# A two-layer fp32 encoder trunk on one core: other routes for weight parts, rotations and sums around TensorE

## The chip, the cores and the metric

The kernel runs on one core of a Trainium2 chip. The core has five engines that each work through a queue of instructions in order: PE (matmul, with its weight loads PEld), DVE (VectorE), ACT (ScalarE), POOL (GpSimd) and SP, which here only issues loads and stores. DMAs are issued from SP's queue (plain loads) or from POOL's (those that add to what lies at the destination). The metric is the time of one execution in microseconds on the device, the median of several runs.

## The reference, cut to what matters

Two layers on x of 512 tokens by 1024, with a memory of 256 tokens, all in fp32. Layer 0 has two token mixers side by side, layer 1 two others (latent attention C, neighbourhood attention D); each layer goes on with cross attention into the memory and a SwiGLU network of width 2816.

```python
def mixer_ab(h, w_in, g_qa, g_ka, sink, w_out, ang_1d, ang_2d):
    qa, ka, va, qb, kb, vb = _split(h @ w_in, AB_SIZES)          # 512,128,128,512,128,128
    qa = apply_rope(rms_norm(qa.reshape(B, S, 8, 64), g_qa), ang_2d)
    ka = apply_rope(rms_norm(ka.reshape(B, S, 2, 64), g_ka), ang_2d)
    oa = blocked_dense_attention(qa, ka, va, HEAD_DIM ** -0.5)   # A: dense
    qb, kb = apply_rope(qb, ang_1d), apply_rope(kb, ang_1d)      # B: no norm
    ob = window_attention_with_sink(qb, kb, vb, sink, HEAD_DIM ** -0.5)
    return jnp.concatenate([oa, ob], axis=-1) @ w_out

for i in range(DEPTH):                                           # 2
    x = x + mixer(rms_norm(x, g_mix[i]))                         # ab, then cd
    x = x + memory_cross_attention(rms_norm(x, g_xq[i]), rms_norm(mem, g_mem[i]), ...)
    g, u = jnp.split(rms_norm(x, g_ffn[i]) @ w_gate_up, 2, axis=-1)
    x = x + (jax.nn.silu(g) * u) @ w_down
return rms_norm(x, g_final)
```

A rotation multiplies a head of 64 by cosines and adds the swapped halves of 32 multiplied by sines. The norm of a head is one factor per token and head, so it may be applied before or after the rotation.

## The kernel before

Every fp32 product is made of three matmuls on a high and a low part of each operand (`mm3`, lines 140 to 142). The high part is the value cast to a shorter format, the low part the rest. So each weight that is loaded (`raw`, by SP) is turned into `wh` and `wl`. `split` (line 117 ACT cast, line 123 subtraction on DVE or, in four pieces, on POOL) does it on the engines. `split_by_dma` (lines 132 to 134) casts the high part, writes the negated value into `wl` with its rounding, and lets a DMA of POOL's queue add the weight from memory to it, which spares the subtraction.

A tile framework orders the instructions of each engine ahead of time by its own simulated schedule; on the chip each engine follows that order and waits on semaphores. PSUM has banks named `mm`, `s`, `t` (two buffers each), `x` and `o` (one each).

Layer 0's mixer (`mixer_ab`): A's keys and values are projected at the start, A's queries and all of B's by `natural`, which fills two `mm` banks for each weight load with 48 matmuls of 256 columns each. `rotate` copies a bank to SBUF (ACT, line 433), squares and sums it for A (POOL line 422, DVE lines 424 and 427), multiplies with cosine on POOL (line 382) and sine on DVE (lines 383 and 384), adds (line 385). The result is cut into high and low (lines 489 and 490), transposed on PE into the one `X` bank (line 447) and copied to a stack by ACT (line 449). Attention runs in units of one head and half of the rows, in three steps (scores, maxima, exponentials; transposes `T` of the weights with ACT line 293 and DVE line 294; products `O`), as a software pipeline (`pipeline`). B's projections are work without waits that the schedule lays between A's attention steps. Then follow two output projections (`out_proj`) and the keys and values of the memory.

The SwiGLU network takes 18 of its 22 column tiles with seven products in place of eight (`left_factors` makes seven left factors from four quarters of a loaded weight, `winograd` multiplies, `pc` and `u` are its partial sums in SBUF, lines 1150 to 1157). Quarters A11, A12 and A22 are themselves left factors (`loaded`, lines 1109 to 1111: two ACT operations and a DMA of 256 KB that adds), four others are sums (`parts`: ACT cast line 1102, DVE subtraction line 1103). Down projections come in three groups (tiles 0 to 7, 8 to 15, 16 to 21). In layer 0 `by_columns` also reorders the tokens of the eight x tiles (ACT line 1172, DVE line 1173). `last_step` makes the final norm in two halves of 256 tokens; the sum of squares is gathered in SBUF and summed over partitions by four small matmuls (line 163).

Of the kernel before, what the change touches and what calls it, by code (L numbers as in the profile page):

```python
# [17 lines left out]
P = 128  # L18
# [13 lines left out]
def trunk_kernel(  # L32
# [30 lines left out]
    def x_bank():  # L63
        return bank_of("X", 1)
# [192 lines left out]
    def softmax_rows(tiles, reduce_max, neg, extra=None):  # L257
# [11 lines left out]
        nc.vector.reciprocal(ri, ssum)  # L269
# [107 lines left out]
    def rope_mul(ph, dst, src, cv, sv, nh):  # L377

        t1 = dst
        t2 = src[1]  # L380
        s = src[0]
        nc.gpsimd.tensor_mul(t1, s, cv)
        nc.vector.tensor_mul(t2[:, :, 0:32], s[:, :, 32:64], sv[:, :, 0:32])
        nc.vector.tensor_mul(t2[:, :, 32:64], s[:, :, 0:32], sv[:, :, 32:64])
        alternate("rot").tensor_add(t1, t1, t2)

    def mixer_ab(after):
# [6 lines left out]
        with tc.tile_pool(name="ab", bufs=2) as ph:  # L394
# [34 lines left out]
            def rotate(src3, scale, cs, tt, nh, norm):  # L429
# [994 lines left out]
```

## Time and profile before

| | us |
|---|---|
| median of 3 runs | 1384.22 (1384.17 to 1385.93) |
| the profiled execution | 1384.54 |
| its span, first to last instruction | 1382.7 |
| PE busy | 1346.1 |
| DVE busy | 981.9 |
| ACT busy | 794.0 |
| POOL busy | 427.9 |

Around the span lie 1.8 us. The mean granted clock of TensorE over the span is 0.993 of full speed. Busy time is the time in which an engine works on some instruction; a busy PE may still work at a lower clock.

### The profile page before, as it was taken

The numbers are of one execution on the slowest core, as the hardware profiler recorded it, in microseconds if no ns is written. First come the engines' busy times: TensorE is split into PE (matmuls) and PEld (weight loads), VectorE is DVE, ScalarE is ACT, GpSimd is POOL, SyncE is SP. The second block draws the span as 40 slices with busy tenths as digits, with TensorE's granted clock in tenths as the row PEclk, the third lists the DMA queues.
The fourth block names the chain that finished last, engine by engine and source line by source line (L and its number), as shares of the span: only waits on it lengthen the run. The fifth ranks groups of instructions, "written<-read, shape, count | busy, mean of one in ns | idle before, by whom it ended". The sixth has DMA issues, their size and how long they took to land.

```text
span 1382.7 us, 24067 instructions
## 1 busy us (share of the span) xinstructions
PE 1346.1 (97%) x9131; PEld 1231.4 (89%) x9131; DVE 981.9 (71%) x1909; ACT 794.0 (57%) x1584; POOL 427.9 (31%) x536
## 2 busy tenths in 40 slices
PE   8998999999999999999999999999999999999997
PEld 8887889998998998898988887798989989998997
DVE  6998886769766785685569656547698766856765
ACT  5467775657643673473468557456567526743543
POOL 4855445212212221210213446642122122212111
PEclk9999999999999999999999999999999999999998
DMA  7110023311862874552222336145207636744721
GB/s 239 62 62 32 1 92 122 123 62 24 198 160 77 199 175 129 133 142 82 79 66 63 73 86 159 38 132 164 72 9 171 173 107 159 179 136 117 181 69 62
DMA packets 98317, 152.45 MB, mean 110 GB/s; under 512 B 7631, under 2 KB 71066, under 8 KB 92570
## 3 DMA queue, kind: packets, MB, share of 16 engines
q1 hardware_dynamic: 77418, 118.93, 26.7%
q0 software_dynamic: 20784, 31.99, 14.2%
q8 instruction: 72, 1.18, 0.3%
q14 instruction: 43, 0.35, 0.1%
HBM read 148.80 MB, written 2.10 MB: 109 GB/s over the span
## 4 chain that ended last, share of the span: by engine, by line
PE 77%; DVE 8%; DMA 6%; ACT 4%; issue 3%; SPq 1%; POOL 1%; POOLq 0%; ACTq 0%; DVEq 0%
PE mm L140 12%; PE mm L141 12%; PE mm L142 12%; PE S L1141 8%; PE mm L1141 5%; PE T L1141 5%; PE O L568 2%; DMA raw<-in_w_gate_up_dram 2%; PE S L140 2%; DMA wl<-in_w_gate_up_dram 2%; PE S L141 2%; PE T L290 2%; PE S L142 2%; PE T L141 1%; PE T L140 1%
## 5 line engine op out<-in xcount | busy, mean ns | idle before, releaser
L117 ACT CAST wh<-raw 128x1024 fp32r<-128x1024 f32 (+3 forms) x125 | 123.0, 987 | 137.2 <-PE mm L141 46.3
L123 DVE TENSOR_TENSOR wl<-raw,wh 128x1024 fp32r<-128x1024 f32 (+3 forms) x115 | 139.8, 1217 | 23.3 <-ACT wh L117 21.6
L271 POOL TENSOR_SCALAR P<-P,sm 128x512 f32<-128x512 f32 (+2 forms) x128 | 82.1, 661 | 79.7 <-DVE sm L269 55.9
L141 PE MATMUL mm<-act,wh 128*128 128x512 f32 (+1 forms) x264 | 98.9, 375 | 0.0
L142 PE MATMUL mm<-act,wl 128*128 128x512 f32 (+1 forms) x264 | 98.7, 375 | 0.0
L1111 POOL DMA_DIRECT2D wh<-in_w_gate_up_dram x54 | 46.9, 868 | 167.1 <-ACT wh L1110 106.1
L140 PE MATMUL mm<-act,wh 128*128 128x512 f32 (+1 forms) x264 | 98.3, 376 | 0.0
L1141 PE MATMUL S<-bf,wl 128*128 128x256 f32 x648 | 87.7, 284 | 1.7 <-DVE pc L1157 1.7
L1141 PE MATMUL S<-bf,wh 128*128 128x256 f32 x648 | 86.2, 283 | 0.0
L1141 PEld LDWEIGHTS S<-bf,wl 128*128 128x128 f32 x648 | 82.0, 192 | 2.4 <-DVE pc L1157 2.1
L1141 PEld LDWEIGHTS S<-bf,wh 128*128 128x128 f32 x648 | 81.9, 192 | 0.5
L1111 POOL DMA_DIRECT2D wl<-in_w_gate_up_dram x54 | 47.2, 873 | 112.8 <-ACT wl L1110 44.1
L1117 DVE TENSOR_TENSOR ws<-raw 128x512 f32<-128x512 f32 x72 | 49.5, 688 | 43.3 <-DMA raw<-in_w_gate_up_dram 43.2
L140 PE MATMUL mm<-wh,xgh 128*128 128x256 f32 (+1 forms) x256 | 74.1, 290 | 3.0 <-ACT rt L433 2.3
L156 POOL TENSOR_TENSOR P<-P 128x512 f32<-128x512 f32 (+1 forms) x21 | 26.3, 1253 | 154.8 <-ACT P L152 154.8
L1102 ACT CAST wh<-ws 128x512 fp32r<-128x512 f32 x72 | 44.6, 619 | 50.2 <-PE mm L141 17.7
L141 PE MATMUL mm<-wl,xgh 128*128 128x256 f32 (+1 forms) x256 | 73.1, 286 | 0.0
L142 PE MATMUL mm<-wh,xgl 128*128 128x256 f32 (+1 forms) x256 | 73.0, 286 | 0.0
L1274 POOL TENSOR_TENSOR x<-x,P 128x512 f32<-128x512 f32 x16 | 24.9, 1559 | 154.8 <-DVE P L1273 154.8
L294 DVE TENSOR_TENSOR ptl<-T,pth 128x512 fp32r<-128x512 f32 (+2 forms) x96 | 58.1, 616 | 14.4 <-ACT pth L293 14.2
L1109 ACT CAST wh<-raw 128x512 fp32r<-128x512 f32 x54 | 33.6, 622 | 53.2 <-PE mm L141 23.6
L293 ACT CAST pth<-T 128x512 fp32r<-128x512 f32 (+2 forms) x96 | 49.5, 536 | 24.8 <-PE T L290 24.4
(424 smaller groups left out, 4754.1 us busy)
## 6 DMA issues: line engine op xcount, KB each, us to landing
raw<-in_w_gate_up_dram SPq DMA_DIRECT2D x44, 1024.0 KB, 5.5
raw<-in_w_down_dram SPq DMA_DIRECT2D x16, 1024.0 KB, 5.6
wl<-in_w_gate_up_dram POOLq DMA_DIRECT2D x54, 256.0 KB, 5.7
wh<-in_w_gate_up_dram POOLq DMA_DIRECT2D x54, 256.0 KB, 5.7
raw<-in_w_xkv_dram SPq DMA_DIRECT2D x8, 1024.0 KB, 5.2
raw<-in_w_down_dram SPq DMA_DIRECT2D x8, 768.0 KB, 5.0
raw<-in_w_in_ab_dram SPq DMA_DIRECT2D x5, 1024.0 KB, 6.5
raw<-in_w_out_ab_dram SPq DMA_DIRECT2D x4, 1024.0 KB, 5.1
```

The source lines that it names most:

```text
L117: nc.scalar.copy(hv, v)
L123: low.tensor_sub(lv[:, q], v[:, q], hv[:, q].bitcast(F32))
L140: nc.tensor.matmul(o, lh, rh, start=start, stop=False)
L141: nc.tensor.matmul(o, lh, rl, start=False, stop=False)
L142: nc.tensor.matmul(o, ll, rh, start=False, stop=stop)
L271: nc.gpsimd.tensor_scalar(p, p, ri[:, j:j + 1], 1.0, op0=ALU.mult, op1=ALU.mult)
L293: nc.scalar.copy(hv, tv)
L294: nc.vector.tensor_sub(ptl[:, k0:k1, j * P:(j + 1) * P], tv, hv.bitcast(F32))
L1102: nc.scalar.copy(hl[:, 0], x)
L1111: nc.gpsimd.dma_start(hl[:, 1], src[:, i], accum_op=ALU.add)
L1117: nc.vector.tensor_tensor(t, x, y, op=op)
L1141: nc.tensor.matmul(bank, x, y, start=start and k == 0 and i == 0, stop=k == n - 1 and i == 2, skip_group_check=True)
```

## The change

Seven edits, in the order of the program. In the rows below a number behind a name tells buffers apart, a row's waits stand in brackets, and line numbers behind the changed helper functions differ by a few between the two kernels.

1. `rotate` takes the sine products directly from the PSUM bank (`scalar_tensor_tensor`, with the token's factor in it), its squares for A by ACT from the bank, and applies the norm after the rotation; POOL's squares go.
2. B's three `natural_weights` take `split_by_dma`: six ACT operations and six DMAs of 512 KB in place of six DVE subtractions. The first of them, for B's keys and values, is issued behind A's last `pow` and last stack copy.
3. `out_proj` in layer 0 splits its even halves on DVE alone and its odd halves by DMA; before, DVE and POOL alternated.
4. `memory_normed` of layer 0 has its squares and their sum behind the exponentials and sums of B's unit 5.
5. A22 is made by `parts` in place of `loaded`.
6. `by_columns` is spread over tiles 16 to 19, two x tiles each.
7. In `last_step` the last two tiles' squares go to the small matmuls without the sum in SBUF before.

```diff
+    def natural_weights(w, c0, eng=None, n=256, by_dma=False):
...
+        return [split_by_dma(v[:, k], 4, n, src[:, k]) if by_dma else split(v[:, k], 4, n, eng) for k in ks]
...
-    def out_proj(os_, w, r0, after=None, by_dma=False):
+    def out_proj(os_, w, r0, after=None):
...
-                if by_dma and mq:
-                    wh, wl = split_by_dma(v[:, :, cq], nk, 256, src[:, :, cq])
-                else:
-                    wh, wl = split(v[:, :, cq], nk, 256, None, nc.vector if by_dma else alternate("op"))
+                wh, wl = split_by_dma(v[:, :, cq], nk, 256, src[:, :, cq]) if mq else split(v[:, :, cq], nk, 256)
...
-            def headnorm(qn, scratch, nh):
-                nc.gpsimd.tensor_mul(scratch, qn, qn)
-                ss = small(nh)
-                nc.vector.tensor_reduce(ss, scratch, axis=AX, op=ALU.add)
-                ri = small(nh)
-                rsqrt_mean(ri, ss, 64, nh)
-                nc.vector.tensor_mul(qn, qn, ri.unsqueeze(2).broadcast_to([P, nh, 64]))
...
+                nc.scalar.activation(v, src, AF.Copy, scale=scale)
+                if norm:
+                    sq = tmp()[:, :nh * 64].rearrange("p (h d) -> p h d", h=nh)
+                    nc.scalar.activation(sq, src, AF.Square, scale=scale)
+                nc.gpsimd.tensor_mul(t1, v, cv)
+                for a, b in ((slice(0, 32), slice(32, 64)), (slice(32, 64), slice(0, 32))):
+                    nc.vector.scalar_tensor_tensor(t2[:, :, a], src[:, :, b], scale, sv[:, :, a],
+                                                   op0=ALU.mult, op1=ALU.mult)
...
-                    natural(xh, xl, w_in, c0, evac)
+                    with tc.issue_after(dense["pow"]), tc.issue_after(dense["stack"]):
+                        parts = natural_weights(w_in, c0, by_dma=True)
+                    natural(xh, xl, w_in, c0, evac, parts)
...
-                natural(xh, xl, w_in, c0, evac, natural_weights(w_in, c0, nc.gpsimd) if isA and c0 == 0 else None)
+                natural(xh, xl, w_in, c0, evac,
+                        natural_weights(w_in, c0, nc.gpsimd if isA and c0 == 0 else None, by_dma=not isA))
...
+        with queued("exp"):
+            for i in range(4):
...
-        r["A22"] = loaded(3)
+        r["A22"] = parts(a22)
...
-                if layer == 0 and j == NF - 2:
-                    by_columns(ph)
+                if layer == 0 and 16 <= j < 20:
+                    by_columns(ph, (2 * j - 32, 2 * j - 31))
...
+        if m < KF - 2:
+            sum_sq(st["acc"], xm, m)
+        else:
+            sq = tmp()[:, :256]
+            nc.scalar.activation(sq, xm, AF.Square)
...
+            for a in (st["acc"], sq) if m == KF - 2 else (sq,):
+                for t in range(2):
+                    nc.tensor.matmul(st["sums"][t], a[:, t * P:(t + 1) * P], ones[:, 0:1],
+                                     start=a is st["acc"], stop=m == KF - 1)
```

How the order moves, first on PE in layer 0's mixer. `mm_759` (before) and `mm_769` (after) are the last bank of A's query projection, `X` the transposes for the stacks, `mm_1516` and `mm_1530` the first bank of B's keys and values. Before:

```order
L141 MATMUL mm_759<-wl_662,xgh_210 128x256
L142 MATMUL mm_759<-wh_661,xgl_211 128x256
L447 MATMUL X_547<-identr_84,nst_514 128x128 [waits DVE_49,Activation_49]
L140 MATMUL mm_1516<-wh_1508,xgh_132 128x256 [waits Activation_49]
L141 MATMUL mm_1516<-wl_1509,xgh_132 128x256
L142 MATMUL mm_1516<-wh_1508,xgl_133 128x256
L140 MATMUL mm_1516<-wh_1508,xgh_142 128x256
```

After, the end of the same projection and what follows:

```order
L141 MATMUL mm_769<-wl_670,xgh_210 128x256
L142 MATMUL mm_769<-wh_669,xgl_211 128x256
L439 MATMUL X_559<-identr_84,nst_518 128x128 [waits Activation_49]
L439 MATMUL X_559<-identr_84,nst_518 128x128 x3
L505 MATMUL S_865<-K_353,Q_457 128x512
L506 MATMUL S_865<-K_353,Q_457 128x512
L505 MATMUL S_869<-K_353,Q_457 128x512
L506 MATMUL S_869<-K_353,Q_457 128x512
```

After, 41 rows further on (five more such pairs of scores are among the rows between), where B's projection begins:

```order
L567 MATMUL O_969<-ptl_920,vst_352 128x256
L140 MATMUL mm_1530<-wh_1520,xgh_132 128x256 [waits Activation_49]
L140 MATMUL mm_1612<-wh_1520,xgh_132 128x256
L141 MATMUL mm_1530<-wl_1521,xgh_132 128x256 [waits DMASW0_49]
L142 MATMUL mm_1530<-wh_1520,xgl_133 128x256
L140 MATMUL mm_1530<-wh_1520,xgh_142 128x256
L141 MATMUL mm_1530<-wl_1521,xgh_142 128x256
```

Before, one stack's transpose stands between A's last projection and B's first, and A's scores come later. After, all of A's stacks, seven pairs of scores (`S`), four groups of transposes (`T`) and a group of products (`O`) stand there, and the second matmul of `mm_1530` waits for a DMA.

On ACT after, where B's first two weight loads (`raw_1518`, `raw_1696`) are turned into parts; `Q_662<-X_859` is A's last stack, `P` are exponentials:

```order
L262 ACTIVATE P_904,sm_910<-S_901,sm_909 128x512 [waits DVE_49,Activation_49]
L441 CAST Q_662<-X_859 128x2x256 [waits PE_49]
L132 CAST wh_1520<-raw_1518 128x1024 [waits DMAHW6_49]
L133 ACTIVATE wl_1521<-raw_1518 128x1024
L132 CAST wh_1525<-raw_1518 128x1024
L133 ACTIVATE wl_1526<-raw_1518 128x1024
L132 CAST wh_1698<-raw_1696 128x1024 [waits DMAHW3_49]
L133 ACTIVATE wl_1699<-raw_1696 128x1024
L132 CAST wh_1703<-raw_1696 128x1024
L292 CAST pth_953<-T_955 128x4x128 [waits PE_49]
L133 ACTIVATE wl_1704<-raw_1696 128x1024
L262 ACTIVATE P_908,sm_910<-S_905,sm_909 128x512 [waits DVE_49,Activation_49]
```

And on POOL after, the DMAs that add to those parts:

```order
L270 TENSOR_SCALAR P_890<-P_890,sm_893 128x512 [waits DMAHW2_49,Activation_49]
L134 DMA wl_1521<-in_w_in_ab_dram 128x4x256 [waits Activation_49]
L134 DMA wl_1526<-in_w_in_ab_dram 128x4x256 [waits Activation_49]
L134 DMA wl_1699<-in_w_in_ab_dram 128x4x256 [waits Activation_49]
L134 DMA wl_1704<-in_w_in_ab_dram 128x4x256 [waits Activation_49]
L270 TENSOR_SCALAR P_904<-P_904,sm_911 128x512 [waits DMAHW1_49,DVE_49]
L270 TENSOR_SCALAR P_908<-P_908,sm_911 128x512 [waits DMAHW3_49,Activation_49]
```

All eight weight operations, with one cast of `pth` among them, stand between A's last stack and the third unit's second exponential; the four DMAs stand ahead of that unit's scaling on POOL. Before, each of these weight pieces has one operation on ACT, one subtraction on DVE and no such DMA.

On DVE around the reordering of tokens, before, where all eight stand among the seven-product tiles (six more are in the 15 rows behind):

```order
L1117 TENSOR_TENSOR ws_7344<-raw_7319,ws_7327 128x512
L1157 TENSOR_TENSOR pc_7080<-pc_7080,S_7078 128x256
L1173 COPY x0_90<-perm_7457 128x512
L1103 TENSOR_TENSOR wh_7208<-ws_7206,wh_7208 128x512
L1223 TENSOR_TENSOR g_7169<-pc_7080,T_7079 128x256
L1173 COPY x1_91<-perm_7460 128x512
L1226 TENSOR_TENSOR g_7169<-pc_7080 128x256
```

And after, where six of them stand among the down projection of the group before (lines 1277 and 1278), and the last two 20 rows further on:

```order
L1278 TENSOR_TENSOR x5_95<-x5_95,P_6832 128x512
L1107 TENSOR_TENSOR wl_6920<-ws_6909,wl_6920 128x512
L1177 COPY x4_94<-perm_7187 128x512
L1177 COPY x5_95<-perm_7190 128x512
L1277 TENSOR_TENSOR P_6866<-mm_6837,bc_4337 128x512
L1107 TENSOR_TENSOR wh_6934<-ws_6932,wh_6934 128x512
L1107 TENSOR_TENSOR wl_6929<-ws_6927,wl_6929 128x512
L1277 TENSOR_TENSOR P_6898<-mm_6869,bc_4337 128x512
L1278 TENSOR_TENSOR x7_97<-x7_97,P_6898 128x512
L1107 TENSOR_TENSOR wl_6937<-raw_6907,wl_6937 128x512
```

The copies moved ahead out of the seven-product tiles; the last row is a low part of A22, which DVE now makes.

## Rows read from the trace of the kernel before

**Rows 1.** the page: span, and busy times by engine

```profile
span 1382.7 us, 24067 instructions
...
PE 1346.1 (97%) x9131; PEld 1231.4 (89%) x9131; DVE 981.9 (71%) x1909; ACT 794.0 (57%) x1584; POOL 427.9 (31%) x536
```

**Rows 2.** the page's chain that ended last, by engine

```profile
PE 77%; DVE 8%; DMA 6%; ACT 4%; issue 3%; SPq 1%; POOL 1%; POOLq 0%; ACTq 0%; DVEq 0%
```

**Rows 3.** waits of PE; line waited for: us in total, times, longest

```profile
PE T L290 <- DVE ptl L294: 3.5, 3, 2.8
...
PE mm L1141 <- DMA wl<-in_w_gate_up_dram: 3.0, 4, 1.3
...
PE mm L140 <- ACT rt L433: 2.3, 2, 2.0
...
PE S L1141 <- DVE pc L1157: 1.7, 2, 0.9
...
PE mm L1141 <- DMA wh<-in_w_gate_up_dram: 0.8, 2, 0.5
...
PE mm L1141 <- ACT pc L1150: 0.8, 1, 0.8
```

**Rows 4.** windows: from:to, length, busy us of PE, PEld, DVE, ACT, POOL; clock, DMA, GB/s

```profile
49.90:61.90 12.00, 9.99 (x70) 9.82 (x70) 10.69 (x24) 3.77 (x8) 10.03 (x12) 0.86 0.28 89
61.90:231.40 169.50, 160.78 (x1165) 147.55 (x1164) 142.48 (x330) 120.78 (x294) 90.40 (x130) 0.98 0.15 51
129.00:136.00 7.00, 6.38 (x31) 5.87 (x32) 6.86 (x16) 4.26 (x10) 4.09 (x7) 0.55 0.47 152
332.00:620.00 288.00, 284.82 (x1958) 265.47 (x1958) 206.42 (x365) 163.07 (x285) 58.26 (x61) 1.00 0.59 148
1050.00:1310.00 260.00, 256.88 (x1777) 240.03 (x1776) 183.15 (x321) 137.18 (x245) 54.19 (x56) 1.00 0.60 151
480.00:500.00 20.00, 20.00 (x169) 20.00 (x168) 17.99 (x37) 14.13 (x28) 5.18 (x6) 1.00 0.76 178
```

**Rows 5.** timeline of PE, where the first mixer's B part begins

```profile
49.63 0.28 PE L447 MATMUL X<-identr,nst 128*128 128x128 f32 x1
...
51.91 0.38 PE L140 MATMUL mm<-wh,xgh 128*128 128x256 f32 x1 [2.01 <-ACT rt L433]
...
59.81 0.47 PE L510 MATMUL S<-K,Q 128*128 128x512 f32 x1
```

**Rows 6.** timeline of ACT, A's first exponential and its last query stack

```profile
62.57 0.69 ACT L263 ACTIVATE P<-S,sm 128x512 f32<-128x512 f32 x1 [0.38 <-DVE sm L274]
...
75.27 0.59 ACT L449 CAST Q<-X 128x512 fp32r<-128x512 f32 x1 [0.67 <-PE X L447]
```

**Rows 7.** one line's instructions, L134: duration ns min/median/max, and its DMAs' landing

```profile
L134 POOL DMA_DIRECT2D wl<-in_w_out_cd_dram x4: 1278/1300/1332, 838.5 to 931.1; - x4
...
DMA to landing us min/median/max: 6.9/8.3/11.5
```

**Rows 8.** timeline of POOL at PE's longest wait

```profile
125.23 2.98 POOL L123 TENSOR_TENSOR wl<-raw,wh 128x256 fp32r<-128x256 f32 x4
```

**Rows 9.** page, costliest groups: count, busy us, mean ns, idle before

```profile
L117 ACT CAST wh<-raw 128x1024 fp32r<-128x1024 f32 (+3 forms) x125 | 123.0, 987 | 137.2 <-PE mm L141 46.3
...
L123 DVE TENSOR_TENSOR wl<-raw,wh 128x1024 fp32r<-128x1024 f32 (+3 forms) x115 | 139.8, 1217 | 23.3 <-ACT wh L117 21.6
...
L1117 DVE TENSOR_TENSOR ws<-raw 128x512 f32<-128x512 f32 x72 | 49.5, 688 | 43.3 <-DMA raw<-in_w_gate_up_dram 43.2
```

**Rows 10.** one line's instructions, L1110: duration ns min/median/max

```profile
L1110 ACT ACTIVATE wl<-raw x54: 625/628/672, 328.2 to 1297.3; 128x512 fp32r<-128x512 f32 x54
```

**Rows 11.** timeline of DVE and PE at the end

```profile
1373.43 0.42 DVE L159 TENSOR_TENSOR P<-P 128x256 f32<-128x256 f32 x1 [0.28 <-ACT P L152]
...
1373.78 0.44 PE L1326 MATMUL T<-identr,P 128*128 128x128 f32 x2 [1.65 <-ACT P L1323]
...
1374.06 0.55 PE L163 MATMUL X<-ones,P 128*128 128x1 f32 x4
```

More of the change, by code (lines that the diff above doesn't have):

```diff
@@ L1 @@
-from contextlib import ExitStack
+from contextlib import ExitStack, nullcontext
 import numpy as np
@@ L146, in rsqrt_mean @@
         marks["mean"] = nc.vector.tensor_scalar(v, src, 1.0 / n, EPS, op0=ALU.mult, op1=ALU.add).ins
-        nc.gpsimd.tensor_tensor(dst, v, mhalf[:, :k], op=ALU.pow)
+        marks["pow"] = nc.gpsimd.tensor_tensor(dst, v, mhalf[:, :k], op=ALU.pow).ins
     def sum_sq(acc, xs_f, f, vec=(1, 3, 5)):
@@ L202, in row_bcast @@
         return bc
-    def natural_weights(w, c0, eng=None, n=256):
-        v = load(w[:, c0:c0 + n].rearrange("(k p) n -> p k n", p=P), KF, n)
-        return [split(v[:, 4 * i:4 * i + 4], 4, n, eng) for i in range(2)]
+    def natural_weights(w, c0, eng=None, n=256, by_dma=False):
+        src = w[:, c0:c0 + n].rearrange("(k p) n -> p k n", p=P)
+        v = load(src, KF, n)
+        ks = [slice(4 * i, 4 * i + 4) for i in range(2)]
+        return [split_by_dma(v[:, k], 4, n, src[:, k]) if by_dma else split(v[:, k], 4, n, eng) for k in ks]
     def natural(xh, xl, w, c0, evac, parts=None, bank_fn=None, n=256):
@@ L268, in softmax_rows @@
             nc.vector.tensor_add(ssum, ssum, es)
-        nc.vector.reciprocal(ri, ssum)
+        marks["sums"] = nc.vector.reciprocal(ri, ssum).ins
         for j, (sb, p) in enumerate(tiles):
@@ L448, in to_stacks @@
                                                 n[:, j, 2 * i + a], identr)
-                    nc.scalar.copy(stacks[i][:, :, b * 256:(b + 1) * 256],
-                                   t.rearrange("p (a n) -> p a n", a=2))
+                    marks["stack"] = nc.scalar.copy(stacks[i][:, :, b * 256:(b + 1) * 256],
+                                                    t.rearrange("p (a n) -> p a n", a=2)).ins
             def kv_part(isA, c0):
@@ L521, in front @@
                             True, sink[:, h:h + 1])
+                        if 2 * h + half == 5:
+                            behind.update(marks)
                 def trans():
@@ L536, in late @@
                 return t[:, 0], t[:, 1]
+            behind, dense = {}, {}
             sa = dict(out=[], Q=[], room=o_tiles)
@@ L552, in mixer_ab @@
             out_proj(sa["out"], w_out, 0)
-            kv_mem.append(memory_kv(0, *memory_normed(0)))
+            kv_mem.append(memory_kv(0, *memory_normed(0, behind)))
             out_proj(sb_["out"], w_out, 512, after)
@@ L861, in mixer_cd, with memory_normed, queued @@
             memory = memory_normed(1)
-            out_proj(sc["out"], w_out, 0, None, True)
+            out_proj(sc["out"], w_out, 0)
             kv_mem.append(memory_kv(1, *memory))
-            out_proj(sd["out"], w_out, 512, after, True)
-    def memory_normed(layer):
+            out_proj(sd["out"], w_out, 512, after)
+    def memory_normed(layer, behind=None):
+        def queued(name):
+            return tc.issue_after(behind[name]) if behind else nullcontext()
         mn = wp.tile([P, 2048], F32, tag="raw", bufs=2, name="mn").rearrange("p (t d) -> p t d", t=2)
@@ L871, in memory_normed @@
         ss, s1, ri = (sm.tile([P, 4], F32, tag="smm", bufs=4, name="smm") for _ in range(3))
-        for i in range(4):
-            junk = gp.tile([P, S], F32, tag="xg", name="junk")
-            nc.scalar.activation(junk, mn[:, i // 2, i % 2 * S:(i % 2 + 1) * S], AF.Square, accum_out=ss[:, i:i + 1])
+        with queued("exp"):
+            for i in range(4):
+                junk = gp.tile([P, S], F32, tag="xg", name="junk")
+                nc.scalar.activation(junk, mn[:, i // 2, i % 2 * S:(i % 2 + 1) * S], AF.Square,
+                                     accum_out=ss[:, i:i + 1])
         sv = ss.rearrange("p (t h) -> p t h", t=2)
-        nc.vector.tensor_add(s1[:, :2], sv[:, :, 0], sv[:, :, 1])
+        with queued("sums"):
+            nc.vector.tensor_add(s1[:, :2], sv[:, :, 0], sv[:, :, 1])
         nc.vector.tensor_scalar(s1[:, :2], s1[:, :2], 1.0 / D, EPS, op0=ALU.mult, op1=ALU.add)
@@ L1166, in columns, with by_columns @@
         return t.rearrange("p (c r) -> p r c", r=8)
-    def by_columns(ph):
-        for f in range(KF):
+    def by_columns(ph, fs):
+        for f in fs:
             t = ph.tile([P, S], F32, tag="oT", bufs=8, name="perm")
@@ L1329, in last_step @@
         if m == KF - 1:
-            rstd = rstd_of(st["acc"], last, nc.vector)
+            rstd = small(2)
+            mean = small(2)
+            for t in range(2):
+                nc.vector.tensor_scalar(mean[:, t:t + 1], st["sums"][t], 1.0 / D, EPS, op0=ALU.mult, op1=ALU.add)
+            nc.gpsimd.tensor_tensor(rstd, mean, mhalf[:, :2], op=ALU.pow)
             for t in range(2):
```

33 lines of the change are left out of this document (15 added, 18 removed).

## The prediction

> **What bounds the kernel now.** I read the page's busy times first: PE works 1346.1 us of a span of 1382.7 [rows 1], so 36.6 us of idle time and the stretches at a lower clock are all that any edit off PE can win. The chain that ended last agrees: PE holds 77% of it, DVE 8%, DMA 6%, ACT 4% [rows 2]. The list of PE's waits then says who was late [rows 3]. Three of its entries belong to edits made here: PE waits 3.5 us for a low part of attention weights (line 294), 2.8 of it at once; 2.3 us for a rotation's copy (line 433), 2.0 at once; and in the SwiGLU network 3.0 and 0.8 us for parts of left factors that a DMA completes. Two more lie beside them: 1.7 us for DVE's partial sums and 0.8 for ACT's. Last I cut the span into windows [rows 4]. From 61.9 (where PE is some way into B's keys and values) to 231.4 (where the second output projection begins) PE is busy for 160.8 of 169.5 us at a mean clock of 0.98: 8.7 us idle, and 0.02 x 160.8 = 3.2 lost to the clock, 11.9 together. The SwiGLU stretches have 3.2 idle us (332 to 620) and 3.1 (1050 to 1310). So the first mixer is where most is to be won, and where most can be lost.
>
> **Part 1: where B's projection starts.** This is the term that I take to decide. Before, PE ends A's last projection at about 49.6, waits 2.01 us and is at work on B's keys and values at 51.91 [rows 5]; A's first scores come at 59.81, the first exponential at 62.57 and the last stack's copy ends at 75.27 + 0.59 = 75.9 [rows 5, 6]. After, A's stacks, seven pairs of scores, transposes and products stand ahead of B's second matmul, which waits for an accumulating DMA. The work moved ahead is some 9 us of PE, the same as PE had done between 49.6 and 61.9 less its waits (9.99 busy, part of it at half clock: mean 0.86), so "61.9 before" and "the second matmul after" are the same state of PE's work. When does the DMA land? Scores start behind A's last projection, at about 50.3. Before, the first exponential came 2.8 us behind them; now DVE has the last banks' rotations ahead of the first maximum, which I estimate at 2.5 us more: exponential at 55.7. From there to the end of the last stack's copy took 13.3 us before (75.9 - 62.57), with B's matmuls and two casts between; without those I estimate 7.5, so 63.2; at the old pace 69. Two operations of 1 us each on ACT make the first low part: a cast of 987 ns in the mean [rows 9] and its like; so 65.2. The DMAs of this form took 6.9 to 11.5 us to land, 8.3 in the median [rows 7]; I take the median: 73.5. PE is then 73.5 - 61.9 = 11.6 us behind. The clock is a further cost: a stretch of 12 us with waits showed 0.86 over 9.99 busy us, a loss of 1.4; the one behind the longest wait showed 0.55 over 6.38, a loss of 2.9 [rows 4]. I take 1.4, because that stretch is the same place.
>
> The Trainium skill, "DMA: Bandwidth & Descriptors", section "Anatomy of one DMA — SWDGE (gpsimd) path", gives 2.0 us plus bytes over 436 thousand per us for such a DMA. For 512 KB that is an estimate of 3.2 us; the row's 8.3 disagrees, and the measurement decides. By the page the matmul would go at 68.4, 5.1 us earlier, and the whole sum below would be 3.5 us under the time before.
>
> **Part 2: the rest of the first mixer.** B's three projections no longer end early: 288 matmuls of 256 columns, 34 us of PE at the 0.118 us that one took elsewhere (20.00 us for 169 [rows 4]), now fill gaps over most of A's attention. The longest wait had POOL on four pieces of a low part for 2.98 us [rows 8] while DVE worked slowly beside it; with odd halves by DMA and even ones on DVE, POOL's pieces go. That names 2.8 of idle and 2.9 of clock, 5.7 of the 11.9; of the other 6.2 I let the fill and DVE's six saved subtractions (1.217 us each, 7.3 in all [rows 9]) remove half. Their price, six more operations on ACT, I put at nothing: ACT is busy for 120.8 of 169.5 there [rows 4], and 6 x 1 us more is 75%; if that cover fails the six cost up to 6. So the stretch takes 169.5 - 11.9 + 3 = 160.6. Sum of parts 1 and 2: 11.6 + 1.4 + 160.6 - 169.5 = **+4.1**. Bounds: with a landing of 6.9, a loss of 1 later and no clock cost, 10.2 + 158.6 - 169.5 = -0.7; with a landing of 11.5, 14.8 + 2.9 + 160.6 - 169.5 = +8.8.
>
> The memory's squares, moved behind B's unit 5, I cost at nothing: they lie beside B's attention on ACT.
>
> **Part 3: A22 and the permutation.** Thirty-six tiles make A22 by a cast and a subtraction: ACT saves 36 operations of 0.63 us [rows 10], POOL 36 DMAs, DVE takes 36 subtractions more of 0.69, the duration of its like of 128 by 512 [rows 9]. The waits for DMAs are those of the matmuls into the `mm` bank, which are A11 and A12's, and both still come by DMA; what helps them is that a third of these DMAs is gone from POOL's queue. I let two thirds of the 3.8 us go: 2.5 (bounds 0 and 3.8). DVE pays: it is busy 17.99 of 20 us in such a stretch [rows 4], two tiles pass in it, so 2 x 0.69 = 1.4 makes 19.4 of 20. It also stands idle 43.2 us for weight loads over the 72 sums [rows 9], so some of it is slack, but its partial sums come later: I add half of their 1.7 us again, 0.8. The permutation's copies stood in front of ACT's late partial sum (0.8 us), and now lie among down projections, where PE has long matmul runs as cover: 0.8 saved. Sum **-2.5**; bounds -5.6 (all DMA and permutation waits and half of DVE's, -3.8 - 0.8 - 1.0) and +3.
>
> **Part 4: the end.** The addition of 0.42 us at 1373.43 no longer stands ahead of the four small matmuls, but the transposes that PE has ahead of them start at 1373.78 anyway [rows 11]; at most 0.5 is won. Each half has 12 small matmul records in place of 4, at 0.14 each (0.55 for four [rows 11]) 1.1 us of PE, in the first half on the path. **0**, bounds -0.5 and +1.1.
>
> **The sum.** 4.1 - 2.5 + 0 = +1.6 on the profiled execution's 1384.54 (span 1382.7 and 1.8 around it), so 1386.1; the median of the runs is 0.3 us below that execution, which I leave in. I call 0.2%, 2.8 us, what a measurement of this kernel can tell from no change.
>
> **The rivals.**
> *The late low part, worse (slower).* The DMA lands at its slowest row, 11.5 us, behind a cold PE: +8.8 - 2.5, 1390.8. For it: ACT issues eight weight operations in one block ahead of the next exponential, and POOL four DMAs at about 1.3 us each [rows 7] ahead of the third unit's scaling, so A's attention itself also stalls. Against: the median is 8.3, and DMA traffic there is low (0.15 of the engines [rows 4]). It decides from a second matmul later than 74.7 us on. The Trainium skill, "SBUF — State Buffer", box on the "DVE blocks DMA" trap, says that descriptors of POOL's DMAs are held up while DVE runs copies in a two-port mode; DVE has copies there, and no row before prices it.
> *The fill pays (faster).* A's chain is short, the DMA lands in 6.9, B's matmuls take up all later waits, and the DMA waits of SwiGLU all go: -0.7 - 3.8 - 0.8 = -5.3, 1379.2; with DVE's waits too, 1377.5. For it: POOL, which worked 10.0 of the 12 us at the start of B [rows 4], loses its squares, and DVE the two-input products from SBUF. Against: PE had enough work there before.
> *DVE becomes the bound of SwiGLU (slower).* At 19.4 of 20 us any late load is no longer made up. A loss of 0.15 us a tile is 36 x 0.15 = 5.4, less the 3.3 won: +4.1 + 2.1, 1390.7. For it: 1.7 us of waits on DVE's sums at 18.0 of 20 already. Against: the idle 43.2 us.
> *The change does nothing to speak of.* A11 and A12 still come late, and the first mixer's gains and losses cancel: 1384.5.
>
> **Chances.** Forecast 0.40 (own range 1382.5 to 1389.5), late low part 0.19, fill 0.20, DVE bound 0.11, nothing 0.10. Faster by over 0.2%: the fill and the lower edge of the forecast and of "nothing", 0.20 + 0.07 + 0.02 = 0.29. Slower: 0.19 + 0.11 + 0.07 = 0.37. The rest, 0.34, is within it. Range: 1377.5 (fill) to 1393.5 (the late low part and DVE's waits at once, 1390.8 + 2.7).
>
> **What would show it.** The wait list after should have B's first matmuls (line 141) waiting for a DMA, at about 62 to 73.5 us, with a clock of one half behind it; the wait for line 294 should be short; no four-piece low part on POOL in the first mixer; DVE at 19 of 20 us and fewer DMA waits in the seven-product tiles; the first `mm` matmul of the second output projection at about 235.5 rather than 231.4. If PE shows no wait of several us ahead of B's projection, part 1 is wrong, and the time is below 1382.

## The result and the profile after

The changed kernel took 1392.78 us in the median of ten runs (1388.73 to 1402.23) against 1384.20 before (1381.71 to 1387.17): a ratio of 1.0068, 95% interval 1.005 to 1.0086. It is slower by about 9 us, beyond the 2.8 us that a measurement can tell, inside the range given (1377.5 to 1393.5) but near its upper end, where the likeliest change was +1.6. Its times also scatter over 13.5 us, where before they scattered over 5.5. The profiled execution took 1392.89 us.

The page's span, busy times and chain that ended last, after (against [rows 1, 2]):

```profile
span 1391.1 us, 23973 instructions
...
PE 1347.9 (97%) x9147; PEld 1232.9 (89%) x9147; DVE 986.7 (71%) x1939; ACT 789.2 (57%) x1570; POOL 388.4 (28%) x480
...
PE 76%; DMA 10%; DVE 7%; issue 4%; ACT 3%; POOL 0%; SPq 0%; POOLq 0%; ACTq 0%; DVEq 0%
```

PE did the same work, 1347.9 us. DMA's share of the chain rose from 6% to 10%.

PE's waits after, in the columns of [rows 3]:

```profile
PE mm L141 <- DMA wl<-in_w_in_ab_dram: 8.9, 2, 6.6
...
PE S L1145 <- DVE pc L1161: 4.5, 4, 2.7
...
PE mm L1145 <- DMA wl<-in_w_gate_up_dram: 2.8, 4, 1.0
...
PE mm L1145 <- DMA wh<-in_w_gate_up_dram: 1.1, 2, 0.6
```

The waits for line 294 and for the rotation's copy are no longer among the large ones. The largest is now the one foreseen in part 1, B's first projection waiting for its low part. In the SwiGLU network the waits for DMAs are 3.9 us (3.8 before), not 1.3, and those for DVE's partial sums have grown from 1.7 to 4.5.

Windows of the kernel after, in the columns of [rows 4]:

```profile
49.90:72.20 22.30, 11.28 (x62) 8.74 (x60) 12.50 (x28) 17.73 (x32) 11.96 (x15) 0.76 0.20 36
72.20:233.90 161.70, 157.17 (x1160) 146.96 (x1161) 124.27 (x306) 117.34 (x280) 82.71 (x113) 0.99 0.36 88
332.00:620.00 288.00, 284.34 (x1951) 264.73 (x1950) 216.44 (x386) 153.70 (x266) 44.47 (x45) 1.00 0.50 131
1050.00:1310.00 260.00, 254.87 (x1758) 238.51 (x1757) 187.58 (x332) 126.34 (x226) 41.43 (x40) 0.99 0.50 131
72.00:79.00 7.00, 4.99 (x27) 4.62 (x27) 2.21 (x5) 2.57 (x7) 2.67 (x3) 0.77 1.12 283
480.00:500.00 20.00, 19.27 (x161) 19.07 (x161) 15.09 (x30) 12.45 (x24) 3.11 (x4) 1.00 0.62 156
```

Up to 72.2 PE had started 409 matmuls, about as many as by 61.9 before (407). From there to the second output projection (233.92 against 231.44) it took 161.6 us in place of 169.5. The first mixer thus ended 2.5 us late. The two SwiGLU windows show 3.7 and 5.1 us in which PE is idle, against 3.2 and 3.1. From 480 to 500, where DVE had been busy for 17.99 us and 19.4 were foreseen, it is busy for 15.09: it has more to do and stands waiting.

The line that makes the sums of quarters (1121, before 1117 [rows 9]) and its idle time until a load landed:

```profile
L1121 DVE TENSOR_TENSOR ws<-raw x72: 680/686/694, 334.9 to 1300.9; 128x512 f32<-128x512 f32 x72
...
  DMA raw<-in_w_gate_up_dram: 61.4, 29
```

DVE stood idle for gate and up loads for 61.4 us against 43.2.

### The profile page after: what moved, and what is told of

Its sections match the earlier page's. It is cut to its first block, busy times and chain, and to the rows that moved or that the text cites. A ratio compares the mean times of both kernels' runs of the same rounds, so it can differ in the third digit from the quotient of the medians.

```text
span 1391.1 us, 23973 instructions
## 1 busy us (share of the span) xinstructions
PE 1347.9 (97%) x9147; PEld 1232.9 (89%) x9147; DVE 986.7 (71%) x1939; ACT 789.2 (57%) x1570; POOL 388.4 (28%) x480
## 4 chain that ended last, share of the span: by engine, by line
PE 76%; DMA 10%; DVE 7%; issue 4%; ACT 3%; POOL 0%; SPq 0%; POOLq 0%; ACTq 0%; DVEq 0%
PE mm L140 13%; PE mm L141 13%; PE mm L142 12%; DMA raw<-in_w_gate_up_dram 6%; PE S L1145 6%; PE T L1145 4%; PE mm L1145 3%; PE O L567 3%; PE T L289 2%; DVE ws L1121 2%; PE S L140 2%; PE S L141 2%; PE S L142 2%; PE T L141 1%; PE T L140 1%
## 5 line engine op out<-in xcount | busy, mean ns | idle before, releaser
L117 ACT CAST wh<-raw 128x1024 fp32r<-128x1024 f32 (+3 forms) x115 | 112.3, 982 | 126.1 <-PE mm L141 41.0
L123 DVE TENSOR_TENSOR wl<-raw,wh 128x1024 fp32r<-128x1024 f32 (+3 forms) x109 | 130.9, 1204 | 32.1 <-ACT wh L117 30.0
L1121 DVE TENSOR_TENSOR ws<-raw 128x512 f32<-128x512 f32 x72 | 49.5, 687 | 61.7 <-DMA raw<-in_w_gate_up_dram 61.4
L1115 POOL DMA_DIRECT2D wh<-in_w_gate_up_dram x36 | 31.5, 874 | 158.4 <-ACT wh L1114 76.3
L1115 POOL DMA_DIRECT2D wl<-in_w_gate_up_dram x36 | 31.6, 878 | 126.3 <-ACT wl L1114 36.2
L141 PE MATMUL mm<-xgl,wh 128*128 128x256 f32 (+1 forms) x192 | 61.2, 321 | 1.1 <-DVE xgl L174 1.1
```

The source lines that it names most:

```text
L117: nc.scalar.copy(hv, v)
L123: low.tensor_sub(lv[:, q], v[:, q], hv[:, q].bitcast(F32))
L141: nc.tensor.matmul(o, lh, rl, start=False, stop=False)
L1115: nc.gpsimd.dma_start(hl[:, 1], src[:, i], accum_op=ALU.add)
L1121: nc.vector.tensor_tensor(t, x, y, op=op)
```

## The experiments

Theories: **(1)** B's first projection waits for an accumulating DMA that is issued too late, and the wait is lost. **(2)** With A22 on DVE the loaded weight's buffer comes free late, so that the next load is late. Rivals: the wait only moves (1); DVE's added work is what costs (2). A run's time stands beside runs of the kernel before on the same chip. "First seven" is the start of PE's first seven-product matmul in the profiled execution against the one before (331.15), thus mostly what happened in layer 0's mixer; "rest" is how much longer than before (1043.2) it took from there to the start of PE's last matmul. These two columns are of one execution each, which can lie some 3 us off the median: a22_alone's was its fastest (1387.53), extra_dve_work's 3.4 us above its median (1388.11). So the medians decide, and the columns only say where.

| label | median us (runs) | ratio, 95% | first seven | rest |
|---|---|---|---|---|
| the change | 1392.78 (10) | 1.0068, 1.005 to 1.0086 | +2.6 | +6.1 |
| a22_alone | 1390.48 (6) | 1.0051, 1.0036 to 1.0065 | -0.5 | +3.6 |
| after_a22_by_dma | 1389.01 (6) | 1.0037, 1.0025 to 1.005 | +5.0 | +1.3 |
| after_kv_split | 1383.76 (11) | 1.001, 0.9993 to 1.0027 | -7.0 | +6.6 |
| after_both | 1377.49 (5) | 0.9956, 0.9944 to 0.9968 | -7.8 | +1.2 |
| extra_dve_work | 1384.69 (11) | 1.0004, 0.9991 to 1.0017 | +0.4 | +3.4 |
| raw_read_by_dve | 1403.79 (4) | 1.0137, 1.0121 to 1.0154 | -2.1 | +23.1 |
| both_old_last_sums | 1376.78 (5) | 0.9954, 0.9941 to 0.9966 | -7.1 | -0.8 |
| permutation_alone | 1383.2 (12) | 0.9993, 0.9984 to 1.0003 | +0.3 | +1.2 |
| rotations_alone | 1371.05 (4) | 0.9903, 0.9888 to 0.9917 | -13.3 | -1.9 |
| out_proj_alone | 1380.61 (8) | 0.997, 0.996 to 0.998 | -5.0 | +2.6 |
| early_kv_dma | 1376.2 (5) | 0.9934, 0.9921 to 0.9947 | -8.6 | +2.1 |
| both_q_split | 1376.52 (6) | 0.9942, 0.993 to 0.9954 | -8.5 | +0.6 |
| rot_and_hold | 1378.86 (6) | 0.997, 0.9959 to 0.9981 | -7.1 | +1.9 |
| rot_and_dma | 1377.12 (6) | 0.9952, 0.9941 to 0.9964 | -6.6 | +2.4 |
| rot_and_out_proj | 1375.28 (5) | 0.9944, 0.9931 to 0.9956 | -11.1 | +2.3 |
| rot_and_memory | 1370.8 (4) | 0.991, 0.9897 to 0.9923 | -11.7 | -1.9 |

**Two repairs, each and both.** The first is the kernel before with A22's line changed; the others start from the changed kernel.

```diff
# a22_alone (on the kernel before)
-        r["A22"] = loaded(3)
+        r["A22"] = parts(a22)
# after_a22_by_dma (on the changed kernel; after_both has this and the next)
-        r["A22"] = parts(a22)
+        r["A22"] = loaded(3)
# after_kv_split (on the changed kernel)
-                        parts = natural_weights(w_in, c0, by_dma=True)
+                        parts = natural_weights(w_in, c0)
```

> The kernel before with A22 alone made by a cast and a subtraction. Theory (A22's subtraction on DVE keeps the weight buffer longer, so the next load is issued later and lands beside the accumulating DMAs): slower than before by 2 to 6 us, DVE idle for gate and up loads about 60 us against 43.2, PE's wait for DVE's partial sums about 4 us against 1.7, and a wider scatter of the times. Rival (fewer DMAs relieve the waits, as the prediction had it): 1 to 3 us faster. Second rival (the loss in the network comes from the spread permutation or the tile phases): no difference beyond 1 us.

> The changed kernel with A22 made by the accumulating DMA as before. Theory (A22 on DVE delays the loads): 3 to 6 us faster than the changed kernel, so 1387 to 1390, DVE's idle time for the loads back to about 43 us, and a narrow scatter. Rival (the network's loss has another cause): 1391 to 1395 with the wide scatter.

> The changed kernel with the first B projection's (keys and values) low parts made by DVE's subtraction, still issued behind A's last stack; the order on PE stays the same up to the second matmul of B. Theory (the wait for the accumulating DMA is lost time): the waits of 6.6 and 2.2 us at that place shrink to about 1, and half clock behind them goes, so 7 to 10 us faster than the changed kernel, 1383 to 1386. Rival (PE meets the same loss a little later, because A's attention and not B's weights bounds the stretch): 0 to 3 us faster, 1390 to 1393.

> The changed kernel with both: A22 by the accumulating DMA, and B's keys' and values' low parts by DVE. If both theories hold and add: 1379 to 1382, faster than the kernel before by 2 to 5. If the wait only moves: 1386 to 1389. If A22 is harmless: as the kernel with the key and value parts alone.

All four moved the way that the two theories had it, two of them beyond the ranges: A22 alone costs 6.8 us, where 2 to 6 were expected, and both repairs are 6.2 us faster than before, where 2 to 5 were. One sign failed: in a22_alone PE waits 0.9 us for `pc`, not 4; its late work there carries other names, DVE's `g` (1.8 us) and ACT's `pc` (1.7). Taking A22 back saves about 4 us in the changed kernel, and 6 beside the other repair (1383.76 to 1377.49). Splitting the keys' and values' weights on DVE saves 9. In the trace of after_kv_split B's first low part holds PE up by a few tenths at most (timeline of PE, start and duration; the second row is the first matmul that needs it):

```profile
66.86 0.40 PE L140 MATMUL mm<-wh,xgh 128*128 128x256 f32 x2
...
67.38 0.39 PE L141 MATMUL mm<-wl,xgh 128*128 128x256 f32 x1
```

**Work or buffer?** Both kernels start from the one before and keep A22 by DMA.

```diff
# extra_dve_work
         r["A22"] = loaded(3)
+        extra = room.tile([P, S], mybir.dt.bfloat16, tag="extra", bufs=1, name="extra")
+        nc.vector.tensor_sub(extra.rearrange("p (k n) -> p k n", k=4), s4, r["A22"][0].bitcast(F32))
# raw_read_by_dve
         r["A22"] = loaded(3)
+        extra = sm.tile([P, 4], F32, tag="extra", bufs=1, name="extra")
+        nc.vector.tensor_sub(extra[:, 0:4].unsqueeze(2), a22[:, :, 0:1], r["A22"][0][:, :, 0:1].bitcast(F32))
```

> The kernel before plus one DVE subtraction of 128 by 512 a seven-product tile, on the high part of A22 and a sum that is in SBUF already; it doesn't read the loaded weight, and A22 still comes by DMA. Its output is thrown away. Theory (A22 on DVE costs because it keeps the loaded weight's buffer): within 1.5 us of before, DVE's idle time for loads falls by about the work added, 43 to some 20. Rival (DVE becomes the bound of the network): 3 to 6 us slower, as with A22 alone.

> The kernel before plus one tiny DVE subtraction (128 by 4) a seven-product tile that reads the loaded A22 and its high part; A22 still comes by DMA, the output is thrown away. The weight's buffer is then given back by DVE's queue and not by ACT's alone, at next to no work. Theory (the buffer's release by DVE delays the loads): slower by 2 to 6 us, DVE's idle time for loads near 60. Rival (it is the 0.69 us of work that costs, or the fewer accumulating DMAs): within 1.5 us of before.

The DVE work alone, with A22's size and place, did not show in the median (+0.7 us, interval -1.2 to +2.4; A22 alone had +5.0 to +9.0), though its profiled execution, the second slowest of eleven, fell 4.2 us behind in the two networks. So the work is free in the median, not in every execution. DVE's idle time for loads was 40.6 us, where I had expected some 20. Its waits and its first SwiGLU window:

```profile
DVE ws L1117 <- DMA raw<-in_w_gate_up_dram: 40.6, 23, 3.5
...
332.00:620.00 288.00, 284.01 (x1952) 264.49 (x1951) 213.83 (x380) 161.53 (x282) 59.28 (x61) 1.00 0.59 148
```

DVE is busy 213.8 us there against 206.4 [rows 4]. A DVE instruction of 128 by 4 that reads the loaded weight costs 19.8 us, where I had expected 2 to 6. The waits of SP, DVE and PE in that kernel (us in total, times, longest):

```profile
SPq L101 <- DVE extra L1133: 487.9, 36, 52.5
...
DVE ws L1117 <- DMA raw<-in_w_gate_up_dram: 60.3, 31, 4.4
...
PE mm L1143 <- DMA wl<-in_w_gate_up_dram: 11.7, 9, 3.9
...
PE mm L1143 <- DMA wh<-in_w_gate_up_dram: 7.1, 6, 2.4
```

The buffers of all 36 seven-product tiles come free only with that tiny instruction. Why it costs so much more than A22 did shows in DVE's timeline:

```profile
457.97 0.69 DVE L1117 TENSOR_TENSOR ws<-raw 128x512 f32<-128x512 f32 x1 [3.48 <-DMA raw<-in_w_gate_up_dram]
...
461.39 0.16 DVE L1133 TENSOR_TENSOR extra<-raw,wh 128x4 f32<-128x4 f32 x1
```

The read at 461.39 stands behind sums that had themselves waited 3.48 us for the next tile's weight, so a late load makes the one after it late. PE then waits for the low parts of A11 and A12 (18.8 us in the two rows of DMAs, against 3.8 before). In this group of tiles, the second of layer 0, the second load starts 8.0 us behind the first before the change and in extra_dve_work, 11.1 in a22_alone and in the changed kernel, and 12.4 here. So what costs is which queue reads the loaded weight last, and at which place in it. How much of A22's own 6.8 us this is, a read placed elsewhere can't say.

**The last sums and the permutation.**

```diff
# both_old_last_sums: after_both, with the two blocks of last_step as in the kernel before
# permutation_alone (on the kernel before)
-                if layer == 0 and j == NF - 2:
-                    by_columns(ph)
+                if layer == 0 and 16 <= j < 20:
+                    by_columns(ph, (2 * j - 32, 2 * j - 31))
```

> The kernel with both repairs (A22 by DMA, key and value parts by DVE) and the last step's sums as before. From the two traces, the last down projection lost 1.1 us and the tail won 0.2: theory (twelve small matmuls stand on PE's path in the first half): 0.5 to 1.5 us faster than with both repairs, 1376 to 1377. Rival (the shorter tail wins): 0.3 to 0.6 slower.

> The kernel before with the token permutation spread over tiles 16 to 19 alone. Prediction's term: 0.8 us faster (1382.9). Rival (ACT's late partial sum was waited for only because other parts were late as well): no difference within 0.7 us.

The old sums were 0.7 us faster than after_both, with intervals that overlap: not settled. The permutation is within 0.2% of before; its 0.8 us, just what the prediction had, can't be told from nothing.

**The mixer's edits one by one.**

```diff
# rotations_alone: the kernel before with the new rotate in place of rope_mul, headnorm and rotate
# out_proj_alone: the kernel before with the new out_proj
# early_kv_dma (on the changed kernel, A22 by DMA)
-                    with tc.issue_after(dense["pow"]), tc.issue_after(dense["stack"]):
-                        parts = natural_weights(w_in, c0, by_dma=True)
-                    natural(xh, xl, w_in, c0, evac, parts)
+                    natural(xh, xl, w_in, c0, evac, natural_weights(w_in, c0, by_dma=True))
# both_q_split (on after_both)
-                        natural_weights(w_in, c0, nc.gpsimd if isA and c0 == 0 else None, by_dma=not isA))
+                        natural_weights(w_in, c0, nc.gpsimd if isA and c0 == 0 else None))
```

> The kernel before with the rotations from PSUM alone. The repaired kernel ended the first mixer 7.9 us earlier than before, and this asks which edit gave it. If the rotations (POOL's squares gone, DVE without two-input products from SBUF): 2 to 5 us faster than before, and PE's wait of 2.0 us for a rotation's copy gone. If they only fill idle engines: within 1.5 us.

> The kernel before with layer 0's output projections alone changed (odd halves by DMA, even ones on DVE, none on POOL). Prediction: the wait of 2.8 us behind POOL's four pieces and the half clock behind it, 5.7 us, go: 3 to 6 us faster than before. If the wait only changes its name: within 1.5 us, with a wait of 2 to 3 us near 126 still there.

> The changed kernel with A22 by DMA and with B's key and value parts by DMA too, but not held behind A's last stack: in the order B's projection then starts right behind A's, as before the change. If it is the place of the DMA that costs, and not the DMA: 1377 to 1381, near the kernel with both repairs. If DMAs of this size in the first mixer cost wherever they stand: 1385 or more, with PE waits for them of several us.

> The kernel with both repairs and B's query weights' low parts also made by DVE, so that no B weight comes by DMA. If the DMA pays for the queries (they are needed late): 1 to 3 us slower than with both repairs, 1378.5 to 1380.5. If DVE had room for four more subtractions: within 1 us of 1377.5.

The rotations alone are 13.4 us faster than before, the fastest with rot_and_memory, far above the 2 to 5 that I expected. Its windows, and then those of the kernel before with the same bounds:

```profile
49.90:61.90 12.00, 12.00 (x102) 11.82 (x102) 11.76 (x26) 6.58 (x13) 10.24 (x11) 1.00 0.26 89
61.90:100.00 38.10, 38.10 (x305) 36.67 (x305) 33.76 (x79) 30.24 (x68) 21.99 (x32) 1.00 0.08 29
100.00:140.00 40.00, 39.52 (x295) 36.07 (x295) 36.11 (x78) 34.46 (x82) 27.47 (x36) 1.00 0.15 54
```

```profile
61.90:100.00 38.10, 36.52 (x294) 34.93 (x293) 35.53 (x75) 25.65 (x58) 24.32 (x34) 1.00 0.08 29
100.00:140.00 40.00, 34.88 (x237) 30.95 (x236) 35.10 (x68) 28.66 (x67) 23.36 (x33) 0.91 0.16 53
```

PE is busy without a gap from 49.9 to 100 at full clock, and the low clock around 130 is gone. The output projections alone win 4.1 us, within the 3 to 6 expected. early_kv_dma differs from after_a22_by_dma in the hold alone, that is, in not issuing the weights of B's keys and values behind A's stacks, and is 12.8 us faster (1376.2 against 1389.01). after_both keeps the hold, makes these weights' low parts on DVE, and is 11.5 faster. So the changed kernel's slow start of B needs both, the hold and the DMA behind it; with only one of them first seven is 8.6 or 7.8 us earlier than before. Without the hold the six DMAs land in 6.0 us in the median, against 10.4 in the changed kernel (DMA issues, first early_kv_dma and then the changed kernel):

```profile
wl<-in_w_in_ab_dram POOLq DMA_DIRECT2D x6, 512.0 KB, 6.0
```

```profile
wl<-in_w_in_ab_dram POOLq DMA_DIRECT2D x6, 512.0 KB, 10.4
```

The query weights by DMA or by DVE make no difference that the intervals show.

**What takes the rotations' gain back.** Each adds one edit to rotations_alone.

```diff
# rot_and_hold
-                    natural(xh, xl, w_in, c0, evac)
+                    with tc.issue_after(dense["pow"]), tc.issue_after(dense["stack"]):
+                        parts = natural_weights(w_in, c0)
+                    natural(xh, xl, w_in, c0, evac, parts)
# rot_and_dma
-                    natural(xh, xl, w_in, c0, evac)
+                    natural(xh, xl, w_in, c0, evac, natural_weights(w_in, c0, by_dma=True))
# (and by_dma=not isA in q_part)
# rot_and_out_proj: the new out_proj
# rot_and_memory: the new memory_normed with its two places in the queues
```

> Rotations from PSUM, and B's key and value weights split on the engines as before but held behind A's last pow and stack copy. Rotations alone were 13.4 us faster than before. Theory (the hold takes PE's only work without waits away while A's chain of rotation, stack and softmax runs): 4 to 7 us slower than rotations alone, 1375 to 1378, with the loss between 50 and 62 us (clock about 0.7). Rival (the hold is free, the DMAs take the time): within 1.5 us of 1371.

> Rotations from PSUM, and all of B's weights' low parts by DMA, with no hold. Theory (without the hold the DMAs land in time): 0 to 3 us slower than rotations alone, 1371 to 1374. Rival (ACT's six more operations and POOL's DMA issues delay A's softmax): 4 us or more slower, 1375 and up.

> Rotations from PSUM, and layer 0's output projections changed. Each alone made the first mixer shorter, by 13.3 and 5.0 us. If they win the same waits: within 1.5 us of rotations alone, 1370 to 1372. If they add: 1366 to 1368.

> Rotations from PSUM, and the memory's squares behind B's unit 5. Prediction: nothing, within 1 us of rotations alone. Rival (they now land where ACT is wanted for B's exponentials and the memory projection): 1 to 4 us slower.

The hold takes back 7.8 us (of the medians; 4 to 7 were expected) even without a DMA. Its window at B's start, and two places of PE's timeline in it:

```profile
49.90:61.90 12.00, 7.77 (x38) 5.87 (x36) 10.05 (x24) 7.69 (x18) 7.45 (x12) 0.73 0.00 1
...
53.13 0.53 PE L440 MATMUL X<-identr,nst 128*128 128x128 f32 x4 [0.76 <-ACT Q L442]
...
56.83 0.79 PE L505 MATMUL S<-K,Q 128*128 128x512 f32 x1 [1.95 <-ACT P L263]
```

PE is busy for 7.77 of 12 us at 0.73 of full speed, where the rotations alone kept it at 12.00 and 1.00: 4.2 us idle and 0.27 x 7.77 = 2.1 of clock, together about the 6.2 by which first seven is later than with the rotations alone. With the low parts by DMA and no hold the loss is 6.1 us, the size that the rival had, not the theory. With the output projections it is 4.2, though these alone were a gain; neither of my expectations for that kernel held. In both PE worked less between 100 and 140 (window, first rot_and_dma, then rot_and_out_proj) than the 39.52 of the rotations alone:

```profile
100.00:140.00 40.00, 37.45 (x259) 33.86 (x257) 35.55 (x70) 31.12 (x72) 23.36 (x30) 0.91 0.09 27
```

```profile
100.00:140.00 40.00, 38.77 (x290) 35.47 (x288) 34.78 (x73) 33.91 (x77) 23.56 (x32) 1.00 0.27 55
```

In rot_and_dma the clock fell there as well, to 0.91: 2.1 us less work and 0.09 x 37.45 = 3.4 of clock are most of the 6.7 by which its first seven is later (its profiled execution, 1380.24, is the slowest of six). rot_and_out_proj's profiled execution loses only 2.2 us up to first seven, and the rest behind it. I can't name one wait for these two losses: the order on every engine is another, and no single entry of the wait lists is large enough. That stays open. The memory's squares cost nothing that the runs show.

## Why the prediction was wrong, step by step

**Part 1, the start of B's projection: right to about a microsecond.** ACT's last stack copy, the first low part, POOL's DMA and PE's wait, in the timelines of the kernel after:

```profile
63.24 0.58 ACT L441 CAST Q<-X 128x512 fp32r<-128x512 f32 x1
...
64.65 1.07 ACT L133 ACTIVATE wl<-raw 128x1024 fp32r<-128x1024 f32 x1
...
66.04 1.49 POOL L134 DMA_DIRECT2D wl<-in_w_in_ab_dram  x1 [3.72 <-ACT wl L133]
...
65.24 0.40 PE L140 MATMUL mm<-wh,xgh 128*128 128x256 f32 x2
...
72.28 0.58 PE L141 MATMUL mm<-wl,xgh 128*128 128x256 f32 x1 [6.64 <-DMA wl<-in_w_in_ab_dram]
...
79.50 0.38 PE L141 MATMUL mm<-wl,xgh 128*128 128x256 f32 x1 [2.23 <-DMA wl<-in_w_in_ab_dram]
```

Forecast: copy's end 63.2, low part 65.2, landing 8.3, matmul 73.5. Measured: 63.8, 65.7, 6.2, 72.3; the landing was shorter and made up for the copy. What was left out is a second wait of 2.2 us at 79.5, for the next low part of the same burst, whose DMA POOL began at 67.92. The clock fell, too, as forecast: it is 0.77 in the mean from 72 to 79, a loss of 0.23 x 4.99 = 1.1 us against 1.4, and the matmuls step by 0.21 us up to 75 and by 0.12 from there.

**Part 2, the rest of the mixer: right in sum, by luck.** 161.6 us against 160.6 and the 1.4 for the clock. The output projections alone won about what I gave them (5.0 of 5.7 by first seven), but on top of the rotations they lost. The large gain comes from the rotations, which the forecast had not priced and only the rival of the fill named: alone they end the mixer 13.3 us earlier, nearly all that PE lost there (11.9 from 61.9 on, and the 2.0 at 49.6 with its clock). The low parts by DMA, costed at nothing on ACT, and the hold took 6 to 8 us each where they were tried on top of it. So the +2.5 at the end of the mixer is a gain of 13 and a loss of 16, not a small loss.

**Part 3, the SwiGLU network: the step that failed.** It was forecast at -2.5. In the change's profiled execution PE's matmuls there fell 1.5 us behind in layer 0 (first +2.6, last +4.1) and 3.1 in layer 1 (+3.8 to +6.9), +4.6 in sum. I counted A22's subtraction as DVE work and let fewer DMAs relieve the waits. The work was indeed free in the median (extra_dve_work). Yet fewer DMAs did not relieve the waits for them (3.9 us, before 3.8). What I did not count is that the subtraction reads the loaded weight, so that the buffer is given back by DVE, and the next load starts only then. In the trace 28 loads of gate and up weights take over the buffer of a seven-product tile. Each starts 0.03 us after DVE ends a subtraction of line 1107 that reads `raw`; before the change each started 0.02 to 0.03 us after ACT ended an operation of line 1110. SP's waits name these lines, too, though line 1107 also makes the other low parts (us, times, longest; the third row is of the kernel before):

```profile
SPq L101 <- DVE wl L1107: 202.1, 8, 53.0
...
SPq L101 <- DVE wh L1107: 101.0, 11, 12.6
...
SPq L101 <- ACT wh L1110: 112.8, 12, 12.2
```

In the second group of layer 0 the next load thus starts 11.1 us behind the first, and before the change 8.0 (timeline of SP, two rows before, two after):

```profile
448.19 0.33 SPq L101 DMA_DIRECT2D raw<-in_w_gate_up_dram  x1
...
456.24 0.33 SPq L101 DMA_DIRECT2D raw<-in_w_gate_up_dram  x1
...
449.59 0.33 SPq L101 DMA_DIRECT2D raw<-in_w_gate_up_dram  x1
...
460.67 0.33 SPq L101 DMA_DIRECT2D raw<-in_w_gate_up_dram  x1
```

And what follows from one late load (timelines of SP, DVE twice around the load, PE):

```profile
1193.98 0.33 SPq L101 DMA_DIRECT2D raw<-in_w_gate_up_dram  x1
...
1193.27 0.68 DVE L1107 TENSOR_TENSOR wl<-raw,wl 128x512 fp32r<-128x512 f32 x1
...
1202.36 0.69 DVE L1121 TENSOR_TENSOR ws<-raw 128x512 f32<-128x512 f32 x1 [3.87 <-DMA raw<-in_w_gate_up_dram]
...
1202.97 0.41 DVE L1161 TENSOR_TENSOR pc<-pc,S 128x256 f32<-128x256 f32 x1
...
1203.43 1.69 PE L1145 MATMUL S<-bf,wl 128*128 128x256 f32 x12 [2.69 <-DVE pc L1161]
```

The subtraction starts at 1193.27, the load at 1193.98, and DVE has nothing to do but wait for it: 3.87 us in front of the sums at 1202.36. The partial sum `pc` stands behind them in DVE's queue, and PE waits 2.69 us for that. This is the longest such wait; the load also took 8.3 us to land, where the median is 5.3, so about 3 us of it come from the landing. So it was neither the forecast nor the rival in which DVE's work is the bound, though the rival's price, 5.4, is near the 4.6 measured. With A22 back on the DMA the changed kernel is about 5 us slower than before, not far from the +3.3 that the forecast has without A22 (4.1 - 0.8): this part is where the sum went wrong. The times scatter over 6.8 to 13.5 us in the three kernels with A22 on DVE, against 4.8 and 2.7 in after_a22_by_dma and after_both; but 23 runs of the kernel before scatter over 8.5. Why they do is not shown.

**Part 4, the end.** PE lost 2.1 us in the last down projection, and 0.6 were won behind it, up to the end of the span: +1.5, against 0 forecast with a bound of +1.1. after_both, with the new sums, shows 1.1 less 0.7; a22_alone, with the old ones, 1.1 less 0.1. So the new sums and A22 each bring about half of it. The sums of small matmuls themselves are within noise.

The forecast's sum was +1.6. Measured in the profile it is +8.4: +2.5 mixer, +4.6 SwiGLU, +1.5 end, and -0.2 in the stretches between. That this lies inside the range is luck too. The upper end was for a late low part and DVE's waits at once, and by the prediction's own terms (+8.8 and +2.1) it should have been 1395.4 and not 1393.5; in part 3's lower bound, half of DVE's 1.7 is 0.9 and not 1.0.

## What to carry to other kernels

Price an edit also by the buffers that it reads: moving the last reader of a loaded tile to a busier in-order queue moves the next load, and nothing of that shows in busy times. Try the parts of a change of many parts one by one, and in pairs; here one edit alone was the fastest, a hold and a DMA cost more together than either alone, and another was a gain alone and a loss on top. Work without waits is worth most beside a chain of dependent small steps; holding it back for the sake of that chain left PE idle and its clock low.

## What the runs showed of the hardware

The sine products of a rotation took 291 to 818 ns with both inputs in SBUF (128 by 128, line 383 before), and 334 to 352 ns with one of them in PSUM (line 423 in rotations_alone, the queries). The first two rows are of the kernel before; at 60.59 no POOL instruction ran:

```profile
L383 DVE TENSOR_TENSOR rt<-rt,q_s x8: 291/447/818, 41.8 to 66.1; 128x128 f32<-128x128 f32 x8
...
60.59 0.28 DVE L384 TENSOR_TENSOR rt<-rt,q_s 128x128 f32<-128x128 f32 x1
```

```profile
L423 DVE SCALAR_TENSOR_TENSOR rt<-mm,sm,tb_s x24: 275/334/346, 61.6 to 126.9; 128x128 f32<-128x128 f32 x16, 128x64 f32<-128x64 f32 x8
...
L423 DVE SCALAR_TENSOR_TENSOR rt<-mm,sm,q_s x16: 334/339/352, 34.0 to 57.6; 128x128 f32<-128x128 f32 x16
```

The Trainium skill, "SBUF — State Buffer", section "Who interferes with whom", says that a DVE instruction with two inputs in SBUF contends with a POOL instruction that reads SBUF, and one with at most one such input, outside the two-port modes, does not. The traces agree: the first form took 0.28 us where POOL stood idle and up to 0.82 where POOL worked on SBUF beside it, and the second kept its duration either way. Whether this is what made the rotations worth 13.4 us is not shown: the same edit also took POOL's squares away and moved the norm, and no run parts them.
